# Written engine order between the output projection and the first feed-forward stages, with the residual mixes in six pieces

## The chip, the cores and the metric

The kernel runs on one core of one Trainium2 chip. The metric is device time in microseconds (us) of one execution. One execution has also been recorded by the hardware profiler; its rows carry times from the span's start. The engines are TensorE (PE: matrix products), VectorE (DVE), ScalarE (ACT), GpSimd (POOL) and SyncE (SP), which here only issues transfers.

## The reference, cut to what matters

One layer of a hybrid encoder: 1024 tokens, width 1024, float32. Three branches (a state-space model, a short convolution, attention) give 512 columns each. The part that matters here:

```python
merged = (gates[:, :, 0] * einsum(y_a, wa) + gates[:, :, 1] * einsum(y_b, wb)
          + gates[:, :, 2] * einsum(y_c, wc))
mix = einsum('bld,de->ble', merged, w_out)
x = x + rmsnorm(mix, g_post_mix)
h = rmsnorm(x, g_pre_mlp)
ff = einsum(square(relu(einsum(h, w_ff1))), w_ff2)      # 1024 -> 4096 -> 1024
return x + rmsnorm(ff, g_post_mlp)
```

## The kernel before

**Products.** Each float32 operand is split into a high part and a low remainder, and each product is made of three matrix products (high by high, high by low, low by high). A weight split is one copy on ACT (the high part, `H` in the names) and one subtraction on DVE (the low part, `L`), both at L73 and L65, written by `split` and `wsplit`. Split weights live in two rings of three buffers (`wH`, `wL`), the loaded float32 weights in a ring of two (`raw`).

**Order of the work around the change.** The 1024 tokens form eight tiles of 128, and two halves `th` of four tiles.

1. `merge_item(th, dp, b)`: the three branch products, gated and summed. An item is two groups of 12 matrix products into one PSUM bank each (`pb`). For each group DVE multiplies with the gate (`gl`), for branches 1 and 2 POOL adds it to the sum `ma`, and after branch 2 the sum is split into `m` (ACT, then DVE). Twelve items per token half: `mg0`, `mg1`.
2. `wo_item`: the output projection into the row accumulators `acc`, four items per half (`wo0`, `wo1`), each of four token tiles by 12 products. The first half of K is copied by ACT (L1262), the second is added by DVE. For the second token half the last two are one item, `wo_last` (products `wl`), tile by tile.
3. `mix(t)` for each token tile: RMS norm of the row, gain and residual added, the sum stored (`x1_s`), a second RMS norm, then eight transposes on PE (`pth`) and the splits into the feed-forward operand. `rms_scale` is a square with a row sum on ACT (L1175) and eight small POOL instructions for the inverse root (L62, names `n_0q`, `n_0r`, `n_0t` for the tile's number). For tiles 0 to 3 the result goes to `h2`; for tiles 4 to 7 to operands `B22`, `T1` to `T4` of a seven-product scheme.
4. The first feed-forward product, stage by stage. Stages 0 to 7 (`prep_a`, `run_a`) make `P1` and `P2` with the weights `wa0` to `wa7`; each is two groups of 12 products and needs only tokens 0 to 3. Stage 8 (`KC`) is the first that needs `T1` and `T2`. The profile calls all these products `P`.

PE takes them in the order mg0, wo0, mg1, wo1, wo_last, stages 0 to 7. The mixes of tiles 0 to 3 fall into mg1, those of 4 to 7 into the end of wo_last and the stages.

**What sets the order.** Two things. First, the program is written as a list by generators: a planner's clock `clk` counts an estimated cost per matrix product (0.214 us), and `spawn` puts a piece of side work into the list as soon as that clock has passed its due time; `poll`, called after each group of 12 products, looks for due pieces. `settle` writes out all that is left. Second, the Tile framework's scheduler reorders the instructions of each engine by its own estimate of when each is ready; semaphores and buffers are handled by it. So the list is a priority, not the order in which an engine works.

`mix(t)` has three pieces before: norm, gain and residual; then (8.0 us of planner's time later for tiles 0 to 3, 9.0 for 4 to 7) second norm, store and gain; then (12.0 later) transposes and splits. For tiles 0 to 3 mix t is spawned when its row is done plus 10.0 times t, for tiles 4 to 7 at once. The residual is added by POOL for tiles 0 to 3 and by DVE for 4 to 7. The row buffer `hr` of tiles 4 and 5 comes from a ring of two in pool `r2`; those of tiles 6 and 7 (`hr67`) lie together in one of the two `raw` buffers.

`run_items` writes the loads one and two items ahead and the weight split of item i+1 ahead of the products of item i. The stage loop writes the weight split two stages ahead (`AH`).

Of the kernel before, what the change touches and what calls it, by code (L numbers as in the profile page):

```python
# [11 lines left out]
F = mybir.dt.float32  # L12
# [8 lines left out]
P = 128  # L21
L = 1024
D = 1024
# [15 lines left out]
def hybrid_layer(ctx, tc, a, out, dbg=None):  # L39
# [24 lines left out]
    def tt(o, x, y, op, eng=None):  # L64
        (eng or dve).tensor_tensor(o, x, y, op=op)  # L65

    def stt(o, i, s, y, op0, op1):
        dve.scalar_tensor_tensor(o, i, s, y, op0=op0, op1=op1)  # L68
# [3 lines left out]
    def split(hi, lo, src, scale=1.0, eng=None):  # L72
        act.activation(hi, src, AF.Copy, scale=scale)  # L73
        if scale == 1.0:
            tt(lo, src, hi.bitcast(F), SUB, eng)
        else:
            stt(lo, src, scale, hi.bitcast(F), MUL, SUB)
# [20 lines left out]
    def spawn(gen, delay=0.0):  # L98
        heapq.heappush(events, (clk[0] + delay, seq[0], gen))
        seq[0] += 1  # L100
# [1072 lines left out]
    def rms_scale(src, jk, name):  # L1173
        sq, rs, tm = small(name + "q"), small(name + "r"), small(name + "t")
        act.activation(jk, src, AF.Square, accum_out=sq)  # L1175
        rsqrt1(rs, sq, tm, pool)
        return rs
# [35 lines left out]
    yT, mT, h2 = {}, {}, {}  # L1213
    macc = {}

    def merge_item(th, dp, b):
        def run(w):
            wh, wl = w[0]
            sl = slice(th * HALF, (th + 1) * HALF)
            if dp == 0 and b == 0:  # L1220
                for kh in range(2):
                    for hl in range(2):
                        mT[hl, th, kh] = big8(f"m{hl}{th}{kh}", [P, 4, HALF])
            if b == 0:
                for d in range(2):
                    macc[d] = mg.tile([P, HALF], F, name=f"ma{th}{dp}{d}", tag="ma", bufs=4)
            yh, yl = yT[th, b]
            for d in range(2):
                dt_ = 2 * dp + d
                gt = mg.tile([P, HALF], F, name=f"gl{th}{dt_}{b}", tag="gl", bufs=4)  # L1230
                sp.dma_start(gt, gt_s[b * 8 + dt_][:, sl])
                ps = mps(f"pb{th}{dt_}{b}")
                ds_ = slice(d * P, (d + 1) * P)
                for ct in range(4):
                    mm3(ps, wh[:, ct, ds_], wl[:, ct, ds_], yh[:, ct, :], yl[:, ct, :], ct == 0, ct == 3)
                if b == 0:
                    stt(macc[d], gt, 1.0, ps, ADD, MUL)
                else:
                    stt(gt, gt, 1.0, ps, ADD, MUL)
                    tt(macc[d], macc[d], gt, ADD, pool)  # L1240
                if b == 2:
                    split(mT[0, th, dt_ // 4][:, dt_ % 4, :], mT[1, th, dt_ // 4][:, dt_ % 4, :], macc[d], scale=0.5)
                yield
        return Item(f"wb{th}{dp}{b}", wb_k[b][:, :, dp * 256:(dp + 1) * 256], [4, 256],
                    [((FULL,), [4, 256])], run)
# [26 lines left out]
    def mix(t):  # L1272

        th = t // 4
        if not mixg:
            mixg.extend([gvec(a["g_post_mix"], "gpost"), gvec(a["g_pre_mlp"], "gmlp")])
        if t == 0:
            for kh in range(2):
                for hl in range(2):
                    h2[hl, kh] = big8(f"h2{hl}{kh}", [P, 4, HALF])  # L1280
        acc = accs[t]
        xr_ = row(f"xr{t}")
        sp.dma_start(xr_, a["x"][t * P:(t + 1) * P, :])
        hr = hrow[0](f"hr{t}")
        rs = rms_scale(acc, hr, f"n1_{t}")
        stt(acc, acc, rs, mixg[0], MUL, MUL)
        tt(acc, acc, xr_, ADD, dve if th else pool)
        yield MY1 if th else 8.0
        rs2 = rms_scale(acc, hr, f"n2_{t}")
        act.dma_start(x1_s[t], acc)  # L1290
        stt(hr, acc, rs2, mixg[1], MUL, MUL)
        c0 = (t % 4) * P
        cs = slice(c0, c0 + P)
        yield MY2 if th else 12.0
        pts = []
        for kh in range(2):
            pt = mps(f"pth{t}{kh}", (P, 4, P))
            for k in range(4):
                kt = kh * 4 + k
                transp(pt[:, k, :], hr[:, kt * P:(kt + 1) * P], ident)  # L1300
            pts.append(pt)
            if not th:
                split(h2[0, kh][:, :, cs], h2[1, kh][:, :, cs], pt)
        if not th:

            if t == 0:
                tk["B11"], tk["D"] = [lt.tile([P, 4, HALF], F, name=n, tag="sa", bufs=2) for n in ("b11f", "bdf")]
            act.activation(tk["B11"][:, :, cs], pts[0], AF.Copy)
            tt(tk["D"][:, :, cs], pts[1], tk["B11"][:, :, cs], SUB)
        else:  # L1310
            for n in ("T2", "T1", "B22", "T3", "T4"):
                if (n, 0) not in tk:
                    for hl in range(2):
                        tk[n, hl] = (ext8 if n in EXTK else big8)(f"{n}{hl}", [P, 4, HALF])

            b12, b22 = pts
            tm = r2.tile([P, 2, 4, P], F, name=f"tm{t}", tag="tm", bufs=2)
            tb = lt.tile([P, 2, 4, P], F, name=f"tb{t}", tag="row", bufs=3)
            act.activation(tb[:, 0], b12, AF.Copy)
            act.activation(tk["B22", 0][:, :, cs], b22, AF.Copy)  # L1320
            tt(tb[:, 1], b12, tk["B11"][:, :, cs], SUB)
            tt(tm[:, 1], b12, tk["D"][:, :, cs], ADD)
            tt(tm[:, 0], b22, tb[:, 1], SUB)
            tt(tb[:, 0], b22, tb[:, 0], SUB)
            stt(tm[:, 1], b22, -1.0, tm[:, 1], MUL, ADD)
            tt(tk["B22", 1][:, :, cs], b22, tk["B22", 0].bitcast(F)[:, :, cs], SUB)
            for n, src in (("T2", tm[:, 0]), ("T1", tb[:, 1]), ("T3", tb[:, 0]), ("T4", tm[:, 1])):
                act.activation(tk[n, 0][:, :, cs], src, AF.Copy)
                tt(tk[n, 1][:, :, cs], src, tk[n, 0].bitcast(F)[:, :, cs], SUB)

    tk = {}
    EXTK = ("B22", "T1", "T2")
    MY1, MY2 = 9.0, 12.0
    WP = (5, 0)
    KC = 8

# [10 lines left out]
    def wo_last(lhs):  # L1347

        src = wo_k[:, 4:8, :]

        def run(w):
            w1h, w1l = woe
            we = [lambda k: (w[k // 2][0][:, k % 2, :], w[k // 2][1][:, k % 2, :]),
                  lambda k: (w1h[:, k, :], w1l[:, k, :])]
            for t in range(4, 8):
                for e in range(2):
                    ps = mps(f"wl{t}{e}")
                    for k in range(4):
                        wh, wl = we[e](k)
                        xh, xl = lhs(t, k)  # L1360
                        mm(ps, xh, wh, k == 0, False, 0.214)
                        mm(ps, xh, wl, False, False, 0.214)
                        mm(ps, xl, wh, False, k == 3, 0.214)
                    dst = accs[t][:, e * HALF:(e + 1) * HALF]
                    tt(dst, ps, dst, ADD)
                    if e:
                        spawn(mix(t))
                    if (t, e) == WP:
                        stages[0][0]()
                    yield  # L1370
        return Item("wol", src[:, :, :HALF], [4, HALF],
                    [((FULL, slice(2 * i, 2 * i + 2), FULL), [2, HALF]) for i in range(2)], run)
# [329 lines left out]
    run_items(mg0[:6], mg0[6:])  # L1702
    yraw = [y_load(1, b) for b in range(3)]
    run_items(mg0[6:], wo0)
    new_acc(range(4), lt)
    for b in range(3):
        run_items(wo0[b:b + 1], wo0[b + 1:] + mg1)
# [5 lines left out]
    new_acc(range(4, 8), lt)  # L1713
    r2_es = ExitStack()
    r2 = r2_es.enter_context(pool_("r2"))
    hlate = []

    def hr_tile(name):
        t = int(name[2:])
        if t < 6:  # L1720
            return r2.tile([P, D], F, name=name, tag="hr", bufs=2)
        if not hlate:
            hlate.append(ws.tile([P, 2, D], F, name="hr67", tag="raw", bufs=2))
        return hlate[0][:, t - 6, :]

    hrow[0] = hr_tile
    stages = ff1_stages()
    run_items(wo1[:1], wo1[1:])
    woe = (ext8("woeh", [P, 4, HALF]), ext8("woel", [P, 4, HALF]))
# [8 lines left out]
    for n, (_, run) in enumerate(stages):  # L1738
        stage[0] = n
        run_due()  # L1740
        if n + AH < len(stages):
            stages[n + AH][0]()
        if n == KC:
            settle()
        to_end = len(stages) - n
        if to_end in (6, 2):
            for k in range(4):
                x_load((0 if to_end == 6 else 4) + k)
        elif to_end == 1:
            for k in range(2):  # L1750
                slice_prep(k)
        for _ in run():
            poll()
        poll()
# [47 lines left out]
```

## Time and profile before

| what | us |
|---|---|
| three runs, median (lowest to highest) | 1704.85 (1703.64 to 1709.92) |
| the profiled execution | 1708.72 |
| its span, first to last instruction | 1707.0 |
| PE busy in the span | 1622.3 (95%) |
| DVE busy | 1029.8 (60%) |
| ACT busy | 693.2 (41%) |
| POOL busy | 499.0 (29%) |

A timeline row reads: start, duration, engine, line of the kernel, operation, output and inputs, shapes, count; in square brackets the idle time of that engine just before, and what ended it. A waits row reads: engine, waiting instruction, what it waited for, then us in total, times, longest. A windows row reads: the stretch, its length, then busy us and instructions of PE, PEld (weight loads), DVE, ACT and POOL, then the granted TensorE clock (1.00 is full), the share of the DMA engines and GB/s. Matrix products overlap: a product's duration is longer than the distance to the next one's start.

### The profile page before, as it was taken

How to read it: one execution, taken by the hardware profiler on the slowest of the kernel's cores; microseconds unless marked ns; L12 is line 12 of the kernel's file. 1: busy time of each engine (PE TensorE's matmuls, PEld its weight loads, DVE VectorE, ACT ScalarE, POOL GpSimd, SP SyncE). 2: the span in 40 equal slices, each digit the busy share in tenths (PEclk: the TensorE clock that was granted, in tenths of full speed). 3: DMA queues.
4: the chain of work that ended last, by engine and by line, in shares of the span. 5: the costliest groups of instructions: out<-in, count | busy, mean ns of one | idle time of the engine just before them, and what ended most of it. 6: DMA issues, size and time to landing. Idle time of an engine off the chain costs nothing.

```text
span 1707.0 us, 21044 instructions
## 1 busy us (share of the span) xinstructions
PE 1622.3 (95%) x7815; PEld 1335.7 (78%) x7815; DVE 1029.8 (60%) x1548; ACT 693.2 (41%) x1042; POOL 499.0 (29%) x603
## 2 busy tenths in 40 slices
PE   7999999999999999997899989699999999999998
PEld 6778778879888787876677768578778878888886
DVE  4768655433264564655564674778888765545565
ACT  4312112231354554555343234554454454443442
POOL 1085643100422303120232552344434300101143
PEclk9999999999999999999899989899999999999999
DMA  5412322330744526331872562356654499755521
GB/s 161 121 41 77 83 86 82 112 93 10 239 152 167 185 75 228 100 142 39 266 250 93 184 223 87 105 161 192 197 189 142 156 334 383 259 198 187 184 99 50
DMA packets 186034, 261.73 MB, mean 153 GB/s; under 512 B 24752, under 2 KB 108764, under 8 KB 183884
## 3 DMA queue, kind: packets, MB, share of 16 engines
q1 hardware_dynamic: 170380, 228.93, 41.9%
q10 hardware_dynamic: 15552, 31.46, 4.9%
q8 instruction: 61, 1.00, 0.2%
q14 instruction: 41, 0.34, 0.1%
HBM read 183.54 MB, written 75.63 MB: 152 GB/s over the span
## 4 chain that ended last, share of the span: by engine, by line
PE 68%; DVE 8%; DMA 4%; POOL 4%; ACT 3%; issue 3%; SPq 1%; DVEq 0%; ACTq 0%; POOLq 0%
PE p_g L122 14%; PE P L122 12%; PE p_q L122 4%; PE pb L122 3%; PE pv L122 3%; PE P4f L122 3%; PE P7f L122 3%; PE P6f L122 3%; PE P5f L122 3%; PE P2f L122 3%; PE P3f L122 3%; PE P1f L122 2%; PE ps L122 2%; PE av L122 2%; PE pt L126 2%
## 5 line engine op out<-in xcount | busy, mean ns | idle before, releaser
L65 DVE TENSOR_TENSOR st<-x,st 128x1024 fp32r<-128x1024 f32 x70 | 86.7, 1251 | 77.5 <-ACT st L73 74.5
L122 PE MATMUL p_g<-hT,w_g_1H 128*128 128x512 f32 x384 | 126.8, 408 | 4.7 <-ACT g L831 3.5
L122 PE MATMUL p_g<-hT,w_g_0H 128*128 128x512 f32 x384 | 126.5, 406 | 2.8 <-DVE ac L65 2.8
L73 ACT ACTIVATE st<-x 128x1024 fp32r<-128x1024 f32 x70 | 73.6, 1059 | 98.5 <-PE P6f L122 16.6
L65 POOL TENSOR_TENSOR w2s<-w2s 128x512 f32<-128x512 f32 x32 | 43.4, 1356 | 228.5 <-DMA w2s<-in_w_ff 219.3
L65 POOL TENSOR_TENSOR s<-w1r 128x512 f32<-128x512 f32 x32 | 52.8, 1671 | 167.0 <-DMA w1r<-in_w_ff 153.7
L65 POOL TENSOR_TENSOR ma<-ma,gl 128x512 f32<-128x512 f32 x32 | 50.0, 1573 | 145.8 <-DVE gl L68 145.8
L122 PE MATMUL pb<-yH,wb_0H 128*128 128x512 f32 x192 | 78.0, 406 | 12.5 <-ACT wb_0H L73 12.5
L122 PE MATMUL pb<-yH,wb_0L 128*128 128x512 f32 x192 | 77.7, 405 | 12.3 <-DVE wb_0L L65 12.3
L65 DVE TENSOR_TENSOR sl<-x,sh 128x1024 fp32r<-128x1024 f32 x42 | 56.6, 1352 | 47.4 <-ACT sh L73 47.4
L122 PEld LDWEIGHTS p_g<-hT,w_g_1H 128*128 128x128 f32 x384 | 69.3, 192 | 17.0 <-ACT g L831 3.9
L122 PEld LDWEIGHTS p_g<-hT,w_g_0H 128*128 128x128 f32 x384 | 70.2, 191 | 15.1 <-DVE ac L65 3.2
L65 POOL TENSOR_TENSOR fa<-fa,gfin 128x512 f32<-128x512 f32 x16 | 25.5, 1606 | 178.0 <-ACT fjk L1644 178.0
L122 PE MATMUL pb<-yL,wb_0H 128*128 128x512 f32 x192 | 77.0, 401 | 0.0
L122 PE MATMUL p_g<-hT,w_g_0L 128*128 128x512 f32 x192 | 76.8, 400 | 0.0
L122 PE MATMUL p_g<-hT,w_g_1L 128*128 128x512 f32 x192 | 76.3, 397 | 0.0
L65 DVE TENSOR_TENSOR PT<-pt,PT 128x512 fp32r<-128x512 f32 (+2 forms) x96 | 53.1, 553 | 32.1 <-ACT PT L73 31.5
L73 ACT ACTIVATE PT<-pt 128x512 fp32r<-128x512 f32 (+2 forms) x96 | 46.9, 489 | 48.5 <-PE pt L126 47.0
L73 ACT ACTIVATE sh<-x 128x1024 fp32r<-128x1024 f32 x42 | 44.2, 1058 | 51.4 <-PE P3f L122 9.9
L1023 ACT ACTIVATE P<-ps,mx 128x128 f32<-128x128 f32 (+3 forms) x64 | 47.3, 740 | 33.1 <-DVE mx L1020 30.7
L1020 DVE TENSOR_REDUCE mx<-ps 128x1 f32<-128x128 f32 (+3 forms) x64 | 48.0, 751 | 13.3 <-PE ps L122 13.1
L122 PEld LDWEIGHTS pb<-yH,wb_0L 128*128 128x128 f32 x192 | 37.5, 195 | 23.2 <-DVE wb_0L L65 15.2
(827 smaller groups left out, 4601.3 us busy)
## 6 DMA issues: line engine op xcount, KB each, us to landing
w2s<-in_w_ff SPq DMA_DIRECT2D x16, 1024.0 KB, 5.0
w1r<-in_w_ff SPq DMA_DIRECT2D x16, 1024.0 KB, 8.6
as<-sa SPq DMA_DIRECT2D x16, 1024.0 KB, 6.7
x<-as SPq DMA_DIRECT2D x32, 512.0 KB, 10.8
x<-t_P SPq DMA_DIRECT2D x32, 512.0 KB, 5.2
r_g<-in_w_in SPq DMA_DIRECT2D x12, 1024.0 KB, 5.8
gt_s<-g ACTq DMA_DIRECT2D x48, 256.0 KB, 2.0
t_P<-w2s SPq DMA_DIRECT2D x48, 256.0 KB, 2.7
```

The source lines that it names most:

```text
L65: (eng or dve).tensor_tensor(o, x, y, op=op)
L73: act.activation(hi, src, AF.Copy, scale=scale)
L122: pe.matmul(o, l, r, start=start, stop=stop)
L126: pe.transpose(o, i, idn)
L1020: dve.tensor_reduce(mx, sv, axis=mybir.AxisListType.XY, op=MAX, negate=True)
L1023: act.activation(Pm[:, 0:kend].rearrange("p (c n) -> p c n", c=nch), sv, AF.Exp, bias=mx, accum_out=sm)
```

## The change

From `new_acc(range(4), lt)`, ahead of wo0, to just before stage 8, the program lies in `tc.manual_schedule` for DVE, ACT, POOL and PE: in it these four engines keep the order of the list. SP is not among them. Four edits go with it: the splits of `m` are spawned 2.0 later instead of standing at once behind the POOL sum; `mix` has six pieces, 1.5, 5.0, 5.0, 5.0 and 2.0 apart, for all tiles alike; mixes 4 to 7 are spawned 0, 4, 8 and 12 after their rows; the residual of tiles 4 to 7 is added by POOL, and so are the low parts of `T3` and `T4`; and all of `hr` for tiles 4 to 7 comes from the ring of two, so that no `raw` buffer is taken for it.

```diff
+    def merged(hi, lo, m):
+        split(hi, lo, m, scale=0.5)
+        yield 0.0
+
@@ merge_item
                 if b == 2:
-                    split(mT[0, th, dt_ // 4][:, dt_ % 4, :], mT[1, th, dt_ // 4][:, dt_ % 4, :], macc[d], scale=0.5)
+                    spawn(merged(mT[0, th, dt_ // 4][:, dt_ % 4, :], mT[1, th, dt_ // 4][:, dt_ % 4, :], macc[d]), 2.0)
@@ mix
         hr = hrow[0](f"hr{t}")
+        yield 1.5
         rs = rms_scale(acc, hr, f"n1_{t}")
+        yield 5.0
         stt(acc, acc, rs, mixg[0], MUL, MUL)
-        tt(acc, acc, xr_, ADD, dve if th else pool)
-        yield MY1 if th else 8.0
+        tt(acc, acc, xr_, ADD, pool)
+        yield 5.0
         rs2 = rms_scale(acc, hr, f"n2_{t}")
         act.dma_start(x1_s[t], acc)
+        yield 5.0
         stt(hr, acc, rs2, mixg[1], MUL, MUL)
         c0 = (t % 4) * P
         cs = slice(c0, c0 + P)
-        yield MY2 if th else 12.0
+        yield 2.0
...
-                tt(tk[n, 1][:, :, cs], src, tk[n, 0].bitcast(F)[:, :, cs], SUB)
+                tt(tk[n, 1][:, :, cs], src, tk[n, 0].bitcast(F)[:, :, cs], SUB, pool if n in ("T3", "T4") else None)
@@ wo_last
                     if e:
-                        spawn(mix(t))
+                        spawn(mix(t), 4.0 * (t % 4))
@@ the body
     run_items(mg0[6:], wo0)
+    ordered = tc.manual_schedule(engines={mybir.EngineType.DVE, mybir.EngineType.Activation, mybir.EngineType.Pool, mybir.EngineType.PE})
+    ordered.__enter__()
     new_acc(range(4), lt)
...
-    hlate = []
-
-    def hr_tile(name):
-        t = int(name[2:])
-        if t < 6:
-            return r2.tile([P, D], F, name=name, tag="hr", bufs=2)
-        if not hlate:
-            hlate.append(ws.tile([P, 2, D], F, name="hr67", tag="raw", bufs=2))
-        return hlate[0][:, t - 6, :]
-
-    hrow[0] = hr_tile
+    hrow[0] = lambda name: r2.tile([P, D], F, name=name, tag="hr", bufs=2)
...
         run_due()
+        if n == KC:
+            settle()
+            ordered.__exit__(None, None, None)
         if n + AH < len(stages):
             stages[n + AH][0]()
-        if n == KC:
-            settle()
```

More of the change, by code (lines that the diff above doesn't have):

```diff
@@ L1328, in mix @@
                 act.activation(tk[n, 0][:, :, cs], src, AF.Copy)
-                tt(tk[n, 1][:, :, cs], src, tk[n, 0].bitcast(F)[:, :, cs], SUB)
+                tt(tk[n, 1][:, :, cs], src, tk[n, 0].bitcast(F)[:, :, cs], SUB, pool if n in ("T3", "T4") else None)
     tk = {}
     EXTK = ("B22", "T1", "T2")
-    MY1, MY2 = 9.0, 12.0
     WP = (5, 0)
```

## The prediction

> **What bounds the kernel now.** I read the page first, then the busy times by stretch, then who PE waits for, then each engine's timeline around the long waits. The profiled execution took 1708.72 us, 1.72 more than its span, and lies 3.87 above the median of the three runs shown (1704.85). The sum below is made inside its span and then taken off the median.
>
> ```profile
> span 1707.0 us, 21044 instructions
> ```
>
> The windows cut the path by PE's own work: wo0; mg1; wo1 with wo_last; stages 0 to 7.
>
> ```profile
> 886.20:931.42 45.22, 44.30 (x193) 35.88 (x192) 25.79 (x24) 15.68 (x21) 9.55 (x12) 1.00 0.34 116
> 931.42:1017.79 86.37, 74.78 (x322) 60.43 (x321) 57.95 (x62) 30.23 (x45) 48.03 (x74) 0.92 0.58 195
> 1017.79:1061.14 43.35, 43.35 (x192) 35.87 (x192) 19.75 (x22) 16.16 (x24) 12.04 (x23) 1.00 0.31 98
> 1061.14:1129.43 68.29, 53.66 (x234) 42.15 (x233) 49.98 (x66) 40.02 (x66) 26.60 (x49) 0.90 0.39 123
> ```
>
> No engine but PE is near full in any of them. What PE would need without waits is counted from its instructions. The chain of waits has 48 products in one dense piece, and a group of eight transposes lasts until the next product starts:
>
> ```profile
> 909.83 10.88 PE wo010p L122 x48
> ```
> ```profile
> 1008.58 1.03 PE L126 MATMUL pth<-ident,hr 128*128 128x128 f32 x8
> 1009.37 0.48 PE L122 MATMUL pb<-yH,wb_0H 128*128 128x512 f32 x1
> ```
>
> So a product costs 10.88 / 48 = 0.2267 and a group of transposes 1009.37 - 1008.58 = 0.79. wo0: 193 x 0.2267 = 43.7, lost 1.5. mg1: 322 less 32 transposes = 290, 65.7 + 4 x 0.79 = 68.9, lost 17.5. wo1 and wo_last: 43.5 of 43.35, nothing lost. Stages 0 to 7: 234 less 32 = 202, 45.8 + 3.2 = 49.0, lost 19.3. Together 38.3 us can be had; that is the ceiling. PE's waits name where they went:
>
> ```profile
> PE P L122 <- DVE wa1L L65: 11.8, 1, 11.8
> PE pb L122 <- DVE wb_0L L65: 11.6, 4, 7.2
> PE P L122 <- DVE wa2L L65: 1.1, 1, 1.1
> PE wo001p L122 <- DVE wo_1L L65: 0.8, 1, 0.8
> ```
>
> In all of them PE waits for DVE's low part of a weight. The losses are larger than the waits (17.5 against 11.6), for after a wait the products stand further apart:
>
> ```profile
> 939.57 0.50 PE L122 MATMUL pb<-yH,wb_0L 128*128 128x512 f32 x1 [2.09 <-DVE wb_0L L65]
> ...
> 941.03 0.63 PE L122 MATMUL pb<-yL,wb_0H 128*128 128x512 f32 x1
> 941.46 0.63 PE L122 MATMUL pb<-yH,wb_0L 128*128 128x512 f32 x1
> ```
>
> 0.43 instead of 0.23, in stretches whose granted clock is 0.92 and 0.90. I price a microsecond of waiting at 17.5 / 11.6 = 1.5.
>
> The Trainium skill (TensorE: Matmul & The Clock Gate, section "Why this matters for your kernels") puts the limit at idle gaps above about 3 us. This trace has a slow spell behind 2.09, so the row decides; by the page's rule shorter waits would cost themselves alone.
>
> Why the low part is late is DVE's order. Before the wait of 7.2 that ended at 992.38:
>
> ```profile
> 982.98 1.05 ACT L73 ACTIVATE wb_0H<-r_wb 128x1024 fp32r<-128x1024 f32 x1
> ```
> ```profile
> 986.17 2.27 DVE L68 SCALAR_TENSOR_TENSOR acc<-acc,n_3r,gpost 128x1024 f32<-128x1024 f32 x1 [2.69 <-POOL n_3r L62]
> 988.37 0.68 DVE L68 SCALAR_TENSOR_TENSOR m<-ma,m 128x512 fp32r<-128x512 f32 x1
> 988.97 3.35 DVE L65 TENSOR_TENSOR wb_0L<-r_wb,wb_0H 128x1024 fp32r<-128x1024 f32 x1
> ```
> ```profile
> 988.52 2.72 POOL L65 TENSOR_TENSOR acc<-acc,xr 128x1024 f32<-128x1024 f32 x1 [1.16 <-DVE acc L68]
> ```
>
> The high part was ready at 984.0, but a mix instruction stood first and waited for POOL; then the low part took 3.35 instead of 1.22, until 988.52 + 2.72 + about 1.1: it ran only after POOL's addition. The same in stage 1, where a whole row of mixes stood first:
>
> ```profile
> 1062.18 1.04 ACT L73 ACTIVATE wa1H<-w1h 128x1024 fp32r<-128x1024 f32 x1
> ...
> 1098.66 0.58 ACT L1461 ACTIVATE s<-P 128x512 f32<-128x512 f32 x1
> ```
> ```profile
> 1076.55 1.29 DVE L68 SCALAR_TENSOR_TENSOR acc<-acc,n_7r,gpost 128x1024 f32<-128x1024 f32 x1 [2.86 <-POOL n_7r L62]
> 1077.75 1.22 DVE L65 TENSOR_TENSOR wa1L<-w1h,wa1H 128x1024 fp32r<-128x1024 f32 x1
> ```
> ```profile
> 1079.07 0.99 SPq L1416 DMA_DIRECT2D w1h<-in_w_ff  x2
> ```
>
> wa1H was ready at 1063.2, wa1L ran at 1077.75, and only then could the next weights be loaded, since `hr67` held the other raw buffer.
>
> **The change part by part.** Prices of a mix's steps:
>
> ```profile
> 925.43 0.19 POOL L62 TENSOR_SCALAR n_0q<-n_0q 128x1 f32<-128x1 f32 x1 [29.80 <-ACT hr L1175]
> ...
> 928.13 0.29 POOL L62 TENSOR_SCALAR n_0r<-n_0t,n_0r 128x1 f32<-128x1 f32 x1
> 929.82 2.40 POOL L65 TENSOR_TENSOR acc<-acc,xr 128x1024 f32<-128x1024 f32 x1 [1.41 <-DVE acc L68]
> ...
> 1004.29 1.29 POOL L65 TENSOR_TENSOR ma<-ma,gl 128x512 f32<-128x512 f32 x1 [1.54 <-DVE gl L68]
> ```
> ```profile
> 924.19 1.06 ACT L1175 ACTIVATE hr<-acc 128x1024 f32<-128x1024 f32 x1 [2.38 <-DVE acc L65]
> ```
> ```profile
> 928.45 1.29 DVE L68 SCALAR_TENSOR_TENSOR acc<-acc,n_0r,gpost 128x1024 f32<-128x1024 f32 x1 [4.29 <-POOL n_0r L62]
> ```
>
> A norm is 1.06 on ACT and 928.42 - 925.43 = 3.0 on POOL, a gain 1.29 on DVE, a residual 2.40 on POOL.
>
> *wo0.* The list puts the split of item i+1 ahead of the evacuations of item i. ACT then holds the evacuations until the weight ring is free, near the end of item i; eight PSUM banks cover that. wo_1L comes first, not behind three copies: the 0.8 goes. The y splits move back into wo0, where DVE is busy 25.8 of 45.2. I keep 0.5 of the 1.5: gain 1.0.
>
> *mg1.* An item is 24 x 0.2267 = 5.44. The low part for the next item is now written a whole item ahead. In front of it on DVE can stand a gate product (0.68), a gain (1.29) and its own worst 3.35: 5.3, just under 5.44. Queued behind a waiting gain are gate products, whose PSUM banks are covered by eight. The steps fit their gaps: 5.0 of the planner are two groups, 5.44 real; a norm needs 4.1, gain and residual 3.7. POOL is the fullest: 16 sums at 1.29, eight norms at 3.0, four residuals at 2.40 make 54 of 69. The spawned splits of m stand one group later in the list, so that ACT, now in order, does not wait at POOL's sum with the next high part behind it. Going through the twelve items by hand I find PE late twice, by about 1 each, where the transposes' splits (three of 0.68) meet a gain. 2 x 1.5 = 3 of the 17.5 stay: gain 14.5; bounds 17.5 (no wait) and 4 (each residual holds up a low part by 2.4, four times, with the clock).
>
> *wo1, wo_last.* ACT waits for woer's load ahead of evacuations; the banks cover it and before had the same chain. Nothing; if that cover fails, one load.
>
> *Stages 0 to 7.* Here the freed raw buffer and DVE's order end the 11.8 and the 1.1. What is late next: the transposes stand in PE's list behind the second group of stages 0, 2 and 4 and the first of 6, and PE can no longer pass them. Per mix PE has two stages, 10.88 + 0.79 = 11.7. In that time POOL has two norms, a residual and the two low parts newly given to it: 6.0 + 2.4 + 2.6 = 11.0. ACT has two weight copies and two squares at 1.06 and twelve copies at 0.58: 11.2. DVE has two low parts at 1.22, two gains at 1.29 and ten at 0.68: 11.8. Three engines as full as PE, in fixed order and waiting for one another, must slip. Worked for tile 5, counting from wo_last's start: transposes of tile 4 end at 28.1; ACT does stage 0's relu and square to 29.3, the six copies of mix 4 to 32.3, wa3H, one evacuation, then the squares of mixes 6 and 5 to 34.9 and 36.1; POOL ends mix 4's low parts at 34.4, the norm of 6 at 37.9, that of 5 at 40.9; the gain ends at 42.1. PE was there at 38.9: it waits 3.2. The same way tile 4 costs 0.2, tile 6 2.2, tile 7 2.6, and stage 9's low part 0.3: 8.5, times 1.5 is 12.8. POOL's residual starts at the moment when DVE's next gain does, in three of the mixes; if POOL is first, DVE waits 2.40. I charge one: 15.2 of 19.3 lost again, gain 4.1. Bounds: gain 19.3 if nothing slips; if POOL is first all three times, (8.5 + 7.2) x 1.5 = 23.5, a loss of 4.2.
>
> The Trainium skill (SBUF — State Buffer, section "Who interferes with whom") has this as a lock: a VectorE instruction with two SBUF inputs and a GpSimd one that reads SBUF exclude each other for the whole instruction, whoever comes first. The 3.35 above agrees. It speaks against moving additions to POOL.
>
> *After stage 8* PE is busy 95% and more either way; I take the saving to last to the end.
>
> Sum: 1.0 + 14.5 + 4.1 = 19.6; 1704.85 - 19.6 = 1685.
>
> **The rivals.** *Nothing slips:* all 38.3, 1666.5. For it: PE's order has slack everywhere in mg1; against: the three engines at 11 of 11.7.
>
> *POOL takes the lock each time in the stages:* 1.0 + 14.5 - 4.2 = 11.3, 1693.5. For it: it was first at 988.52; against: DVE's next instruction needs no signal where the rate was ready earlier.
>
> *The same:* the waits only change names, mg1 keeps 13.5 and the stages lose 4.2: 4 + 1 - 4.2, or the block does not reorder what matters: 1704. Against: the rows above are plain inversions of the list.
>
> *Slower:* SP is not in the block. A weight load stands behind gate loads in its queue, and those wait for POOL's sums to free their buffers, now in order behind norms and residuals.
>
> ```profile
> 980.92 6.78 SPq L1231 DMA_DIRECT2D gl<-gt_s  x2
> 991.27 0.33 SPq L1283 DMA_DIRECT2D xr<-in_x  x1
> 992.38 0.38 SPq L1188 DMA_DIRECT2D r_wb<-in_w_branch  x1
> ```
> ```profile
> 998.00 1.06 ACT L73 ACTIVATE wb_0H<-r_wb 128x1024 fp32r<-128x1024 f32 x1 [4.63 <-DMA r_wb<-in_w_branch]
> ```
>
> It happened here once: ACT stood 4.63. If the eight items with POOL sums each did, 37 comes in and mg1's 17.5 goes: with wo0's 1.0 and the stages' 4.1 the time is 1704.85 + 37 - 22.6 = 1719. It decides where POOL runs over 7.5 later than I reckon: item 4's last sum ends 31.6 after mg1's start, the load behind it takes 998.00 - 992.38 = 5.6, and ACT wants it at 44.7.
>
> **How the numbers follow.** A run of this kernel tells about 0.5% (8.5 us) from no change. The forecast has 0.50 (1676 to 1693, its own range: mg1 and the stages each off by some 5); nothing slips 0.10; the lock 0.13; the same 0.14; slower 0.13. Faster: 0.73. The range 1667 to 1702 takes in the first three and half of the fourth.
>
> **What would show it.** Right: PE's wait for wa1L gone, the mg1 stretch 69 to 73 long, the stages' stretch some 64 with waits of 2 to 3 named after the transposes' input from DVE, wa2's load tens of us earlier. Wrong: PE waits in mg1 for low parts whose high part waits on a load (slower), or no wait at the transposes (nothing slips).

## The result and the profile after

The changed kernel takes 1724.38 us (median of four runs, 1722.92 to 1727.81), the kernel before on the same chip 1707.38. The ratio is 1.0095 (95% interval 1.0078 to 1.0113): slower, where 1685.0 and faster was forecast. The profiled execution took 1727.81.

```profile
span 1726.1 us, 21008 instructions
```

First the windows, cut as in the prediction: wo0; mg1; wo1 with wo_last; stages 0 to 7. The last one ends where stage 7 does; before, it held nine products more, of stage 8, which the scheduler had put ahead.

```profile
890.88:934.40 43.52, 43.52 (x193) 36.04 (x192) 23.07 (x23) 22.04 (x26) 4.23 (x8) 1.00 0.33 112
934.40:1018.24 83.84, 73.77 (x321) 59.33 (x320) 61.31 (x63) 29.43 (x44) 60.17 (x78) 0.96 0.58 196
1018.24:1061.76 43.52, 43.52 (x193) 36.04 (x192) 17.05 (x18) 17.60 (x25) 10.43 (x21) 1.00 0.36 109
1061.76:1144.21 82.45, 57.04 (x225) 46.54 (x224) 58.44 (x55) 36.14 (x60) 50.52 (x63) 0.81 0.34 109
```

wo0 loses nothing any more (45.22 before). mg1 got 2.5 shorter (86.37 before), not 14.5. The stages got 14 longer (68.29 before), at a granted clock of 0.81. By the prediction's reckoning of PE's own work, mg1 has 289 products and four groups of transposes, 68.7, and loses 15.2; the stages have 193 and four groups, 46.9, and lose 35.5 where they lost 19.3. PE's waits, from wo0 to behind the stages:

```profile
PE pth L126 <- DVE hr L68: 31.9, 6, 8.8
PE pb L122 <- DVE wb_0L L65: 2.7, 2, 2.2
```

The waits for low parts of weights (11.8 and 11.6 before) are nearly gone. In their place PE waits for the normed row `hr`, at the transposes. PE's timeline at the transposes of tiles 4 to 7:

```profile
1070.56 1.97 PE L126 MATMUL pth<-ident,hr 128*128 128x128 f32 x8 [3.19 <-DVE hr L68]
...
1094.12 1.94 PE L126 MATMUL pth<-ident,hr 128*128 128x128 f32 x8 [8.82 <-DVE hr L68]
...
1115.44 1.94 PE L126 MATMUL pth<-ident,hr 128*128 128x128 f32 x8 [8.04 <-DVE hr L68]
...
1132.60 1.97 PE L126 MATMUL pth<-ident,hr 128*128 128x128 f32 x8 [5.36 <-DVE hr L68]
```

They come 23.6, 21.3 and 17.2 apart, where PE's own work for one mix is 11.7. What fills those 23.6 is read from the other engines between the rows of tiles 4 and 5. ACT:

```profile
1060.20 1.04 ACT L73 ACTIVATE wa2H<-w1h 128x1024 fp32r<-128x1024 f32 x1
1070.67 0.60 ACT L1467 ACTIVATE s<-P 128x512 f32<-128x512 f32 x1 [9.43 <-DVE hr L68]
...
1073.78 0.60 ACT L1326 ACTIVATE tb<-pth 128x512 f32<-128x512 f32 x1 [0.46 <-ACT o L1413]
...
1079.86 1.05 ACT L1175 ACTIVATE hr<-acc 128x1024 f32<-128x1024 f32 x1
...
1080.89 1.05 ACT L1175 ACTIVATE hr<-acc 128x1024 f32<-128x1024 f32 x1
```

The evacuation `s` of stage 0 goes into the buffer of tile 4's accumulator (`tag="acc0"` at L1464), so it waits until DVE has written tile 4's normed row from it; ACT, in order, stands 9.43. Then come the copies of tile 4's transposes, and only then the squares of tiles 6 and 5, though tile 5's residual was added long before. POOL:

```profile
1067.08 2.34 POOL L65 TENSOR_TENSOR acc<-acc,xr 128x1024 f32<-128x1024 f32 x1
1078.08 1.76 POOL L65 TENSOR_TENSOR T<-tb,T 128x512 fp32r<-128x512 f32 x1 [8.66 <-ACT T L1335]
...
1081.64 1.04 POOL L62 TENSOR_SCALAR n_6q<-n_6q 128x1 f32<-128x1 f32 x1
...
1085.57 0.19 POOL L62 TENSOR_SCALAR n_5q<-n_5q 128x1 f32<-128x1 f32 x1
...
1086.14 2.39 POOL L62 TENSOR_SCALAR n_5t<-n_5r,n_5q 128x1 f32<-128x1 f32 x1
...
1090.56 2.34 POOL L65 TENSOR_TENSOR acc<-acc,xr 128x1024 f32<-128x1024 f32 x1
```

And DVE, at the end of this chain:

```profile
1090.63 3.34 DVE L68 SCALAR_TENSOR_TENSOR hr<-acc,n_5r,gmlp 128x1024 f32<-128x1024 f32 x1 [2.15 <-POOL n_5r L62]
```

Read downwards: tile 4's row, stage 0's evacuation, tile 4's copies, tile 6's first norm, tile 5's second norm (5.0 instead of 3.0, one step of it 2.39 instead of 0.34), tile 5's row (3.34 instead of 1.29, beside the residual that POOL began 0.07 earlier). One tile after the other goes through ACT, POOL and DVE, and PE stands in order behind each.

From wo1's first product to stage 8's first product with the third weight (P with `T` and `wb_1H`) before took 123.4 and after takes 140.0: 16.6 longer. The medians differ by 17.0 and the two profiled spans by 19.1; between the two profiles wo0 and mg1 together are 4.2 shorter, wo0 begins 4.7 later, and the rest lies behind the stages. I use the stretch from wo1 on, "the stages" below, and mg1's to compare the runs. In the code ahead of wo0 the change only moves the splits of `m` in mg0, and the profiles differ there by some us (wo0 began between 884.5 and 890.9 in the runs below), so differences of 2 or 3 between single profiles mean little.

### The profile page after: what moved, and what is told of

Read it like the earlier page. It is cut to its first block, busy times and chain, and to the rows that moved or that the text cites. A ratio compares the mean times of both kernels' runs of the same rounds, so it can differ in the third digit from the quotient of the medians.

```text
span 1726.1 us, 21008 instructions
## 1 busy us (share of the span) xinstructions
PE 1630.0 (94%) x7815; PEld 1342.2 (78%) x7815; DVE 1040.0 (60%) x1536; ACT 693.7 (40%) x1042; POOL 531.3 (31%) x615
## 4 chain that ended last, share of the span: by engine, by line
PE 64%; DVE 9%; POOL 6%; issue 5%; ACT 4%; DMA 3%; SPq 1%; ACTq 0%; DVEq 0%; POOLq 0%
PE p_g L122 14%; PE P L122 7%; PE pb L122 5%; PE p_q L122 3%; PE pv L122 3%; PE P4f L122 3%; PE P7f L122 3%; PE P3f L122 3%; PE P6f L122 3%; PE P5f L122 3%; PE P2f L122 3%; PE P1f L122 2%; PE ps L122 2%; PE av L122 2%; DVE sa L65 2%
## 5 line engine op out<-in xcount | busy, mean ns | idle before, releaser
L73 ACT ACTIVATE st<-x 128x1024 fp32r<-128x1024 f32 x70 | 73.6, 1059 | 98.6 <-PE P6f L122 16.6
L122 PEld LDWEIGHTS pb<-yH,wb_0H 128*128 128x128 f32 x192 | 37.1, 193 | 22.3 <-ACT wb_0H L73 15.0
## 6 DMA issues: line engine op xcount, KB each, us to landing
x<-as SPq DMA_DIRECT2D x32, 512.0 KB, 10.8
```

The costliest lines, as they stand in the source:

```text
L122: pe.matmul(o, l, r, start=start, stop=stop)
```

## The experiments

mg1 and "stages" are stretches of the profiled run, cut at first products and good to 0.2; "waits" are PE's at the transposes of tiles 4 to 7. "And" means on top of the row above.

| run | median | ratio to before (95%) | mg1 | stages | waits |
|---|---|---|---|---|---|
| before | | | 86.2 | 123.4 | 0 |
| after | 1724.4 | 1.0095 (1.0078 to 1.0113) | 83.8 | 140.0 | 25.4 |
| order in mg1 only | 1710.4 | 1.0017 (1.0004 to 1.0029) | 84.5 | 125.5 | 16.0 |
| order in the stages only | 1723.5 | 1.0089 (1.0068 to 1.0110) | 81.6 | 140.7 | 24.6 |
| edits, no order | 1710.0 | 1.0008 (0.9993 to 1.0024) | 81.6 | 126.8 | 15.0 |
| order, no edits | 1750.0 | 1.0245 (1.0225 to 1.0264) | 103.0 | 147.5 | 0 |
| after with the residuals 4 to 7 on DVE | 1720.5 | 1.0064 (1.0040 to 1.0089) | 85.2 | 135.6 | 23.8 |
| and low parts on DVE | 1714.4 | 1.0030 (1.0017 to 1.0043) | 84.1 | 130.7 | 20.1 |
| before with the row ring | 1712.6 | 1.0019 (1.0002 to 1.0037) | 86.2 | 126.7 | 9.3 |
| after with the transposes later | 1717.4 | 1.0050 (1.0031 to 1.0070) | 84.3 | 137.2 | 19.7 |
| after with s1 elsewhere | 1719.2 | 1.0059 (1.0038 to 1.0081) | 84.4 | 137.0 | 23.8 |
| and second norms earlier | 1707.9 | 1.0000 (0.9986 to 1.0014) | 83.9 | 126.3 | 14.7 |
| and additions 4 to 7 on DVE | 1706.4 | 0.9987 (0.9973 to 1.0000) | 83.8 | 124.4 | 15.0 |
| and residuals 0 to 3 on DVE | 1704.4 | 0.9976 (0.9961 to 0.9991) | 81.0 | 124.5 | 15.1 |
| and rows 4 to 7 earlier | 1701.1 | 0.9959 (0.9946 to 0.9971) | 81.5 | 122.6 | 13.5 |
| and splits of m later | 1700.5 | 0.9949 (0.9934 to 0.9964) | 78.6 | 122.6 | 13.8 |
| before, ring and s1 elsewhere | 1711.4 | 1.0024 (1.0013 to 1.0035) | 84.7 | 131.0 | 10.8 |

**Where does the loss sit?** Four runs cut the change in two ways.

```diff
# order in mg1 only: the written order ends ahead of the second half's accumulators
     settle()
+    ordered.__exit__(None, None, None)
     new_acc(range(4, 8), lt)
# order in the stages only: it begins there
     settle()
+    ordered = tc.manual_schedule(engines={...})
+    ordered.__enter__()
     new_acc(range(4, 8), lt)
# edits, no order: neither line; order, no edits: both lines, in the kernel before
```

> The block ends after mg1; from wo1 on the scheduler orders the engines, with the new mixes. Theory: the loss of the change lies in stages 0 to 7, where PE in list order waits for the gain of each of tiles 4 to 7 ahead of its transposes (3.19 + 8.82 + 8.04 + 5.36 us); ordered wo0 and mg1 by themselves bring 1.5 + 2.3 us. It expects those four waits to fall below 8 together and 1698 to 1708. Rival: the order in wo0 and mg1 delays what follows, or a cost spread over the program: 1715 or more.

> The block begins only behind mg1. Theory: the whole loss is here, the four waits ahead of the transposes are as in the changed kernel (25 us together) and the time is 1720 to 1730, a little above the changed kernel's since mg1's small gain is gone. Rival (the order of mg1 is at fault): under 1712.

> All edits but no written order: six pieces, later spawns, residual and two low parts on POOL, hr from the ring. Theory: the fixed order makes the loss; without it PE's transposes are put where their input is ready, and the time is 1695 to 1712. Rival: the edits make it, above all the additions given to POOL, which hold up DVE's gains: 1716 or more.

> The kernel before with the written order alone: mixes in three pieces 9 and 12 apart, residual of tiles 4 to 7 on DVE, hr67 in a raw buffer. Theory: the transposes are written 12 behind the gain, so PE does not wait for them (under 5 us together), but DVE waits in order for POOL's norms inside a piece and PE for low parts behind it: 1705 to 1720. Rival (fixed order as such costs, whatever the spacing): 1722 or more, with waits at the transposes as in the changed kernel.

The order from wo1 on gives the whole loss, the order ahead of it next to none, and the edits alone leave the time where it was. With the order in mg1 only, the waits at the transposes are 16.0, not under the 8 that I expected, and the time lies above the 1698 to 1708: the scheduler's order of the new mixes has such waits too. With the edits and without the order in it mg1 is 81.6, with both (and POOL's additions as the change has them) 83.8 to 85.2: there the edits shortened mg1, not the order. The order without the edits costs 42: that is the rival's time, but the waits at the transposes that the rival named are not there. Its waits in PE's view:

```profile
PE pb L122 <- ACT wb_0H L73: 14.2, 3, 6.4
PE pb L122 <- DVE wb_0L L65: 8.4, 4, 4.0
PE P L122 <- ACT wa1H L73: 7.7, 1, 7.7
```

So the order needs the edits. Which of them makes it bearable, the six pieces, the later splits of `m` or the free `raw` buffer, these runs don't separate. In the run of the edits without the order PE waits from wo1 on mainly for

```profile
PE pth L126 <- DVE hr L68: 15.0, 2, 8.4
```

The 11.8 at `wa1L` moved to the transposes of tiles 5 and 6.

**Is it POOL's additions?**

```diff
-        tt(acc, acc, xr_, ADD, pool)
+        tt(acc, acc, xr_, ADD, dve if th else pool)
# and in the second run also
-                tt(tk[n, 1][:, :, cs], src, ..., SUB, pool if n in ("T3", "T4") else None)
+                tt(tk[n, 1][:, :, cs], src, ..., SUB)
```

> The changed kernel with one line different: the residual of tiles 4 to 7 is added by DVE instead of POOL, as in the kernel before; the written order and everything else stay. Theory 1 (the lock: each of the gains of tiles 4 to 6 took 3.35 instead of 1.29 because POOL's residual of 2.34 ran beside it, 3 x 2.06 = 6.2 on the chain, and POOL's short norm steps of 0.2 to 0.3 took up to 2.4): the gains come back to 1.3, PE's waits at the transposes fall from 25 to 10 to 15, and the time from 1724 to 1706 to 1714. Theory 2 (a mix is a chain through ACT, POOL and DVE, each in order, and its length does not hang on who adds the residual): the waits stay at 20 to 25 and the time at 1718 to 1726. Rival 3 (DVE, now with 1.29 more for each mix, becomes the bound): slower than 1726, with waits for low parts of the weights.

> As the run before it, and the low parts of T3 and T4 on DVE again too, so that POOL has only the norms' short steps in the stages. Theory 1 (lock): no gain and no norm step is lengthened at all, waits at the transposes under 10, 1700 to 1708. Theory 2 (the chain in order): the norm of the next mix starts 2.6 to 3.5 earlier on POOL, but the two low parts stand ahead of the next gain on DVE (2 x 0.68 or so): waits 18 to 24, 1716 to 1724. Rival 3 (DVE the bound: 11.8 + 1.3 + 1.4 = 14.5 for each mix against PE's 11.7): the transposes' waits change into waits for low parts, 1720 or more.

The residual's return gives 4, as the second theory had it; with the low parts it is 10, between the two theories and nearer to the second. In the second of these runs DVE's and POOL's rows for tile 5 are

```profile
1084.46 1.28 DVE L68 SCALAR_TENSOR_TENSOR hr<-acc,n_5r,gmlp 128x1024 f32<-128x1024 f32 x1 [1.86 <-POOL n_5r L62]
```
```profile
1078.99 2.39 POOL L62 TENSOR_SCALAR n_5t<-n_5r,n_5q 128x1 f32<-128x1 f32 x1
```

The row is back at 1.28, yet waits of 20.1 stay: POOL's additions, by the lock and by POOL's time, are a part of the loss and not the whole. The two runs don't tell the lock's share from that of the time. (A norm step of POOL still takes 2.39 beside two DVE instructions with two SBUF inputs each, which ran from 1078.91 to 1081.34.)

**Does the position of the transposes do it?**

```diff
-        yield 2.0
+        yield 5.0 if th else 2.0
-                        spawn(mix(t), 4.0 * (t % 4))
+                        spawn(mix(t), 5.0 * (t % 4))
```

> The changed kernel with the transposes of tiles 4 to 7 one group of 12 products later in the list (last gap 5.0 instead of 2.0, and the mixes begin 5.0 instead of 4.0 apart, which the ring of two needs). Same instructions, written order. Theory 1 (PE in order meets a late chain: a fixed delay): each mix has 2.7 more before its transposes and 1.1 more after the mix before it; the four waits of 3.2, 8.8, 8.0 and 5.4 shrink to 1, 4, 2 and 0, the time to 1702 to 1710. Theory 2 (throughput: ACT, POOL and DVE together need 17 to 24 for each mix however the list puts them): the waits shrink by 4 to 6 in all, 1715 to 1720.

7 less, and the waits 25.4 to 19.7, as the second theory had it: the rows themselves come later still.

**Does the row ring alone take the wait at `wa1L`?** It was what I had named, with DVE's order, as that wait's cause.

```diff
# in the kernel before: hr67 goes
-    hrow[0] = hr_tile
+    hrow[0] = lambda name: r2.tile([P, D], F, name=name, tag="hr", bufs=2)
```

> The kernel before with one part of the change: the normed rows of all tiles go through the ring of two, so the second raw buffer isn't held by those of tiles 6 and 7. No written order, mixes in their old pieces. Theory A (as I had it in the prediction: the held buffer and DVE's order together made the wait of 11.8 at wa1L; the buffer alone lets the weights of stage 1 be split before the mixes): wait gone or under 4, 1694 to 1700. Theory B (DVE's order made it, the buffer had no part, or the ring of two makes the square of tile 6 wait for the transposes of tile 4, so that the wait moves to the transposes): 1704 to 1712, with waits of 6 to 9 at the transposes as in the run of the edits without the written order.

```profile
PE pb L122 <- DVE wb_0L L65: 11.7, 4, 7.2
PE pth L126 <- DVE hr L68: 9.3, 2, 5.6
```

The wait at `wa1L` goes, as theory A had it, so the held buffer was needed for it. But 9.3 at the transposes comes, and the time is theory B's within 1. With a ring of two the square of tile 6 has to wait for the transposes of tile 4; the `raw` buffer that `hr67` held had let all four mixes run through at once (their rows at 1063.0, 1072.4, 1082.4 and 1086.6 before).

**The chain itself.** First s1's buffer is untied from the mixes, with the same list in the stages; then the second norms stand earlier in it.

```diff
-                s1t[i // 2] = lt.tile([P, 2, HALF], F, name=f"s1_{i}", tag=f"acc{(i // 2) % 4}")
+                s1t[i // 2] = (r2 if i // 2 % 5 == 0 else lt).tile([P, 2, HALF], F, name=f"s1_{i}", tag=("s1x", "acc0", "acc1", "acc2", "acc3")[i // 2 % 5])
# the tm ring has one buffer instead of two. In the second run also, in mix
-        yield 5.0
+        yield 2.0 if th else 5.0
         rs2 = rms_scale(acc, hr, f"n2_{t}")
         act.dma_start(x1_s[t], acc)
-        yield 5.0
+        yield 8.0 if th else 5.0
```

> The changed kernel with the evacuations of the stages' first groups (s1) in other buffers: the first pair of stages gets a spare row of its own, the following ones the accumulator one tile earlier (the spare row is taken from the ring of tm, one buffer instead of two). In the changed kernel stage 0's evacuation goes into the buffer of tile 4's accumulator, so ACT stands 9.4, 8.0 and 4.9 until DVE has written that tile's normed row, and everything behind it on ACT (the copies of the transposes, the square of the next tile) stands too. The order of PE, DVE and ACT in the stages stays as it was. Theory 1 (this buffer ties the mixes together): ACT's waits at s1 go, the transposes' waits fall from 25 to 10 or 15, 1706 to 1714. Theory 2 (the list itself ties them: the copies of tile t and the norm of tile t+2 stand ahead of the second norm of tile t+1): waits 17 to 23, 1714 to 1722.

> As the run before it, and in the mixes of tiles 4 to 7 the second norm is put earlier in the list (gap after the residual 2.0 instead of 5.0, gap before the normed row 8.0 instead of 5.0), so that it stands ahead of the copies of the tile before and of the first norm of the tile after; through the planner's steps the transposes of some tiles come one group later too. POOL still adds the residuals and the two low parts. If both ties hold (buffer and list): waits at the transposes under 8, 1698 to 1706. If only the buffer counts: as the run before it, within 4. If POOL's lock and load are the bound: 1712 or more, with gains of 3.35 in front of the waits.

With s1 elsewhere ACT no longer waits for it, but for the next thing in its list:

```profile
1061.86 0.60 ACT L1467 ACTIVATE s<-P 128x512 f32<-128x512 f32 x1 [3.43 <-PE P L122]
1068.31 0.63 ACT L1412 ACTIVATE o<-o 128x512 f32<-128x512 f32 x1 [5.85 <-DVE o L65]
```

DVE's `o` stands behind tile 4's row in DVE's list, so the tie is there twice, by the buffer and by the order; 5 of the loss went, which is the second theory's time. With the second norms ahead of the copies of the tile before, 11 more went: 1707.9, all of the change's loss, with POOL's additions still as the change has them. PE at the transposes in this run:

```profile
1068.61 1.13 PE L126 MATMUL pth<-ident,hr 128*128 128x128 f32 x8 [2.03 <-DVE hr L68]
...
1083.77 1.94 PE L126 MATMUL pth<-ident,hr 128*128 128x128 f32 x8 [4.25 <-DVE hr L68]
...
1103.23 1.94 PE L126 MATMUL pth<-ident,hr 128*128 128x128 f32 x8 [6.13 <-ACT hr L1175]
...
1116.67 1.39 PE L126 MATMUL pth<-ident,hr 128*128 128x128 f32 x8 [2.31 <-DVE hr L68]
```

The time lies just above the 1698 to 1706 that I expected, and the waits are above the 8. In this run some transposes also stand a group later, which by itself (with wider spacing) had given 7; the norms' own share of the 11 is not separated from that. The earlier norms with s1 in its old buffer were not tried: in that order, as I read the list, the engines would wait for one another in a circle.

**Is anything left in POOL's additions, then?**

```diff
-        tt(acc, acc, xr_, ADD, pool)
+        tt(acc, acc, xr_, ADD, dve if th else pool)     # and low parts of T3, T4 on DVE; next run:
+        tt(acc, acc, xr_, ADD)                          # all eight residuals on DVE
```

> As the run before it, and the residuals of tiles 4 to 7 and the low parts of T3 and T4 are added by DVE. Undoing these in the changed kernel gave 10 us. If the lock's price is on the chain still: 5 to 10 less than the run before it, 1692 to 1700. If the chain has slack now, the same as the run before it within 3. If DVE is the bound (14.4 for each mix against PE's 11.7): slower than the run before it by 3 to 8, with waits for low parts of the stages' weights.

> As the run before it, and the residuals of tiles 0 to 3, in mg1, by DVE too: POOL loses 4 additions of 2.4 to 3.4, DVE gets 4 of 1.2. Theory 1 (in mg1 POOL, in written order, is what PE ends up waiting for: residual between two sums, ACT behind the sum, next high part behind ACT; and the lock lengthens both): the stretch of mg1 falls from 84 to 75 to 79, and the time by 5 to 9 against the run before it. Theory 2 (POOL's norms and its 16 sums are enough to keep it the bound, or the loss is ACT's order): the stretch stays at 82 to 84, the time within 3.

1.9 in the stages and 1.6 in the time, where the same edits had given 10 with the old chain. The chain has slack there now: the two cures remove the same waits, so their gains don't add. The residuals of tiles 0 to 3 give 2.8 in mg1's stretch and 2.0 in the time, nearer to the second theory. POOL's share of mg1 falls from 60 to 48 of 81, and mg1 hardly follows: POOL's load was not what bound it.

**What still keeps the rows back?**

```diff
# rows 4 to 7 earlier
-        yield 8.0 if th else 5.0
+        yield 5.0
         stt(hr, acc, rs2, mixg[1], MUL, MUL)
-        yield 2.0
+        yield 5.0 if th else 2.0
# and splits of m later
-                    spawn(merged(..., macc[d]), 2.0)
+                    spawn(merged(..., macc[d]), 6.0)
```

> As the run with all residuals on DVE, and the normed row of tiles 4 to 7 is put 3.0 earlier in the list (gap before it 5.0 instead of 8.0, gap before the transposes 5.0 instead of 2.0), with the transposes where they were. In that run POOL had tile 5's second norm ready at 1071.7, but DVE wrote the normed row only at 1083.8, behind the low part of stage 4's weight and behind the gain and residual of tile 6, and PE waited 9.8 there and 4.6 at tile 6. If the list alone keeps the row back: DVE writes it about 5 to 7 earlier, the two waits fall to 3 or less together, 1690 to 1698. If ACT's and DVE's work for each mix is the bound (throughput): the waits move to the weights' low parts or the next transposes, 1700 to 1706.

> As the run before it, and the copy and split of m begin 6.0 instead of 2.0 of the planner behind POOL's last sum (in mg0 and mg1). In mg1 ACT, in order, stands up to 7 at these copies, whose input POOL has not summed yet, with the next weight's high part and the next square behind them; DVE's normed row of tile 3 stands behind m's low part. If this ties mg1's engines together: the stretch of mg1 falls from 81 to 72 to 76, tile 3's wait of 5.1 goes, and the time falls by 5 to 9 against the run before it. If POOL itself is late: the same within 3, with POOL waiting for nothing in mg1.

In the run before these, POOL's last step for tile 5 and DVE's row:

```profile
1071.41 0.29 POOL L62 TENSOR_SCALAR n_5r<-n_5t,n_5r 128x1 f32<-128x1 f32 x1
```
```profile
1083.76 1.28 DVE L68 SCALAR_TENSOR_TENSOR hr<-acc,n_5r,gmlp 128x1024 f32<-128x1024 f32 x1
```

and with the row earlier in the list:

```profile
1074.16 1.28 DVE L68 SCALAR_TENSOR_TENSOR hr<-acc,n_5r,gmlp 128x1024 f32<-128x1024 f32 x1
```
```profile
1075.58 1.56 PE L126 MATMUL pth<-ident,hr 128*128 128x128 f32 x8 [3.96 <-ACT o L1413]
...
1098.04 1.94 PE L126 MATMUL pth<-ident,hr 128*128 128x128 f32 x8 [8.87 <-DVE hr L68]
```

Counted from stage 0's first product (at 1057.11 in the first of these profiles, at 1054.21 in the second), the row comes 6.7 earlier, and tile 5's wait falls from 9.84 to 3.96, but tile 6's grows from 4.63 to 8.87. The list did keep tile 5 back, as the first theory had it, but most of the wait moved on, and the time, 3 less, is the second's. The later splits of m give 2.9 in mg1's stretch, less than the 5 to 9 expected, and the time stays within 1. What is left there is once more a matter of the list, here tile 3's second norm. POOL, DVE and PE in that run:

```profile
987.01 4.53 POOL L65 TENSOR_TENSOR ma<-ma,gl 128x512 f32<-128x512 f32 x2 [3.02 <-DVE gl L68]
991.63 0.19 POOL L62 TENSOR_SCALAR n_3q<-n_3q 128x1 f32<-128x1 f32 x1
```
```profile
994.64 2.27 DVE L68 SCALAR_TENSOR_TENSOR hr<-acc,n_3r,gmlp 128x1024 f32<-128x1024 f32 x1 [3.21 <-POOL n_3r L62]
```
```profile
996.96 1.10 PE L126 MATMUL pth<-ident,hr 128*128 128x128 f32 x8 [3.54 <-DVE hr L68]
```

The norm's input was ready when ACT's square ended at 987.6; POOL did two sums first. This last version takes 0.9949 of the kernel before (0.9934 to 0.9964), the best of all runs.

**Does the tie need the written order?** The kernel before with the ring and with s1 elsewhere:

> The kernel before, no written order, with the normed rows in the ring of two (as in the earlier run of that alone, which gave 1712.6) and the s1 evacuations in other buffers (as above). If s1's buffer ties the mixes together whatever sets the order: the waits of 5.6 and 3.7 at the transposes shrink and the time falls to 1700 to 1706. If the tie needs the written order (the planner already lets ACT do other work while s1 waits): 1709 to 1714, no change.

1711.4 against 1712.6 with the ring alone: no change. Where the scheduler sets ACT's order, s1's buffer costs nothing that these runs show.

## Why the prediction was wrong, point by point

*wo0* held: 1.7 gained, 1.0 forecast. *wo1 and wo_last* held: 43.52 against 43.35. The predicted traces came too: the wait at `wa1L` is gone, that low part ran at 1062.57 instead of 1077.75, and the load of `wa2`'s weights was issued at 1041.19 instead of 1079.07.

*mg1* failed at "I find PE late twice, by about 1 each". PE was late five times, by 5.51, 2.21, 0.95, 0.88 and 0.52: 10.1, times the 1.5 of the prediction 15.1, and 15.2 were lost. The price was right and the list of waits was wrong. Its largest member is the same that I had seen in the stages and not looked for here: transposes in PE's list that PE can no longer pass, while POOL's sums stand ahead of the norm. For tile 3 two sums came between ACT's square, done at 994.1, and POOL's norm, which began at 996.48; POOL had it ready at 1001.0, but DVE wrote the row only at 1003.55, behind the low part of `m`. "POOL is the fullest", 54 of 69, was right as a sum and of little use: taking 12 off POOL gave 2.8.

*Stages 0 to 7* failed at the reckoning of the four waits, 0.2 + 3.2 + 2.2 + 2.6. They were 3.19 + 8.82 + 8.04 + 5.36. For tile 5 I had the squares of tiles 6 and 5 end 36.1 behind wo_last's start, and the row 6.0 after that. The trace has the squares end at 1081.9, 41.9 behind that start (1040.0), and the row 12.0 after them. The first part, 5.8 late, comes from tile 4's row (its transposes end 4.4 later than reckoned: a norm of 5.8 instead of 3.0 and a row of 3.35 instead of 1.29) and from the copies, which I ran without DVE between them; and I had ACT evacuate stage 0 ahead of tile 4's row, which its buffer forbids. The second part, 6.0 more, is POOL's low parts at 1.75 instead of 1.29, two norms of 3.8 and 5.0 instead of 3.0 and the row's 3.34: the lock, which I had charged once in all and only between residual and gain. It came at the rows of all four tiles (3.35, 3.34, 3.35 and, beside a weight sum, 2.27), and in the norms. Then the error of each tile carried over to the next, since a tile's second norm stands behind the copies of the tile before; I had worked each tile against PE's undelayed time.

The price was 35.5 / 25.4 = 1.4 for a microsecond of wait, near the 1.5.

The sum's deeper fault is the shape of the comparison. Before, the four mixes ran past PE in 24 us and cost one wait of 11.8. In written order each of them stands in PE's list, so PE pays four times for the chain's length. I counted the busy time of each engine for one mix (11.0, 11.2, 11.8 of 11.7) and called it slack or slip; a chain that goes ACT, POOL, DVE, PE, ACT is as long as the sum of its links, not as the fullest of its engines.

*The rivals.* The lock each time, at 1693.5, named the right place and the right engine, but took mg1's gain for granted and the lock for the whole. The slower rival, at 1719, was near in time and wrong in cause: in mg1 of the changed kernel none of the engines' waits is for a DMA, so the weight loads behind SP's gate loads did no harm.

The Trainium skill (SBUF — State Buffer, sections "SBUF: two separate sides" and "Who interferes with whom") says that a VectorE instruction with two SBUF inputs and a GpSimd one that reads SBUF shut each other out for the whole instruction. The rows agree, in both directions and down to GpSimd's 128x1 steps: 2.39 instead of 0.34 beside two DVE instructions that ran from 1086.05 to 1088.48. By that rule the change could have been read as a risk for every norm in the stages, not for the residuals alone.

## What to carry to other kernels

Before fixing an order by hand, follow one whole round of the side chain through every engine's list, with buffer reuse (who must have read what before this write) as links of the chain, and compare its length, not its busiest engine, with the time that the main engine has for it. Where side work for item t+1 stands behind the finish of item t on any engine, the items run one after the other. Here that round took 17 to 24 us against 11.7 of PE's own work, and PE waited in each of the four. A cure tried alone and with others tells whether two cures remove the same wait: here 10 and 16.5 made 18 together.

## What the hardware showed that I had not expected

Whether a wait costs more than itself doesn't follow from its length alone. PE's timeline in mg1 of the changed kernel:

```profile
959.92 0.50 PE L122 MATMUL pb<-yH,wb_0L 128*128 128x512 f32 x1 [2.21 <-DVE wb_0L L65]
...
961.02 0.63 PE L122 MATMUL pb<-yH,wb_0L 128*128 128x512 f32 x1
961.45 0.63 PE L122 MATMUL pb<-yH,wb_0H 128*128 128x512 f32 x1
```

Behind 2.21 the products stood 0.43 apart, from 960.59 to 963.58. Behind 0.52 in the same profile they kept 0.23, and so they did behind 1.52 in the run with all residuals on DVE. But they also kept 0.23 behind 2.19, at the same place in the run with the order in mg1 only:

```profile
956.16 0.50 PE L122 MATMUL pb<-yH,wb_0L 128*128 128x512 f32 x1 [2.19 <-DVE wb_0L L65]
956.50 0.40 PE L122 MATMUL pb<-yH,wb_0H 128*128 128x512 f32 x1
956.74 0.40 PE L122 MATMUL pb<-yL,wb_0H 128*128 128x512 f32 x1
```

And in the kernel before with the row ring they stood 0.43 apart behind only 1.46:

```profile
1117.69 0.50 PE L122 MATMUL P<-h,wa6L 128*128 128x512 f32 x1 [1.46 <-DVE wa6L L65]
...
1118.63 0.63 PE L122 MATMUL P<-h,wa6L 128*128 128x512 f32 x1
1119.06 1.06 PE L122 MATMUL P<-h,wa6H 128*128 128x512 f32 x2
1119.91 0.63 PE L122 MATMUL P<-h,wa6L 128*128 128x512 f32 x1
```

Two windows of that run, up to this wait's end and behind it, and one up to the end of the 2.19:

```profile
1114.00:1117.60 3.60, 1.82 (x7) 0.86 (x5) 3.60 (x4) 0.00 (x0) 2.27 (x2) 1.00 0.30 108
1117.69:1121.20 3.51, 3.51 (x10) 2.77 (x11) 0.82 (x2) 2.36 (x4) 3.51 (x3) 0.59 0.00 0
```
```profile
952.50:956.10 3.60, 1.48 (x7) 0.90 (x5) 3.60 (x3) 1.15 (x3) 2.52 (x2) 1.00 0.59 221
```

Behind the 1.46 the granted clock was 0.59. PE had been busy for 1.82 of the 3.60 up to it, and for only 1.48 of 3.60 up to the end of the 2.19, which no slow spell followed. So neither the length of a wait nor the work just ahead of it parts the two here; what does stays open. The Trainium skill (TensorE: Matmul & The Clock Gate, section "Why this matters for your kernels") puts the limit at idle gaps of about 3 us; here slow products came behind 1.46, 2.09 (the row in the prediction) and 2.21 and none behind 2.19, and the rows decide. So the factor of 1.5 is a mean over waits that cost themselves alone and waits that cost more.

The slow spell doesn't begin at once, either. In the last version, behind the wait of 3.54 at 996.96, the eight transposes took 1.10 and two more products were at full rate; from 998.74 on they stood 0.43 apart. In the changed kernel the transposes behind 3.19 and more took 1.94 to 1.97.
